# A list scheduler's prices are made anew: a port that GpSimd and VectorE share, waits within an engine, and TensorE's changes of shape

## The chip, the core and the metric

The kernel runs on one core of one Trainium2 chip. A core has a TensorE (PE) for matmuls, which writes only to PSUM; a VectorE (DVE), a ScalarE (ACT) and a GpSimd (POOL) for the rest of the arithmetic; and a SyncE (SP), which here issues every DMA. Each engine works through its own instructions in the order in which the program gives them, and semaphores hold an instruction until what it needs is there. The metric is the device time of one run of the whole program in microseconds, as the median of several runs.

## The reference

A two-layer trunk over 2048 latent tokens and 256 context tokens of width 1024, all in float32. Layer 0 has gated linear attention (GLA, chunks of 64, both directions) beside a gated linear recurrence (RG-LRU); layer 1 has windowed attention beside a chunked retention. Cut to its core:

```python
for i in range(DEPTH):                                   # 2 layers
    mod = silu(c) @ ada_w[i] + ada_b[i]                  # shift, scale and gate; the same map for c_ctx
    hl = rms_norm(x, norm_g[i]) * (1 + sc_l) + sh_l      # latent tokens
    hc = rms_norm(ctx_h, norm_g[i]) * (1 + sc_c) + sh_c  # context tokens
    if i % 2 == 0:                                       # GLA || RG-LRU
        q, k, v, g_gla, lr, xr, g_lru = split_cols(h @ w_in, EVEN_SIZES)
        b = cumsum(log_sigmoid(lr @ gla_up + gla_b) / 16) # within a chunk, both directions
        att = where(mask, (q * exp(b)) @ (k * exp(-b)).T, 0)
        S = decay[..., None] * S + k_st.T @ v             # from chunk to chunk
        o = att @ v + (q * exp(b)) @ S
        xc = conv(xr); r, ig = sigmoid(xc @ wa), sigmoid(xc @ wx)
        h_t = a_t * h_{t-1} + sqrt(1 - a_t**2) * ig * xc  # a = exp(8 r log_sigmoid(lam))
    else:                                                # windowed attention || retention
        p = softmax([q @ k.T in a window of +-128, q @ kc.T, sink]);  o = p @ [v, vc]
        o_ret = the chunked form above with one fixed decay for each head
    y = concat(branch outputs * silu(gates))
    x = x + g_l * (y @ w_out)
    ctx_h = ctx_h + g_c * (y_c @ w_out)                  # after layer 0 only
out = rms_norm(x, final_g)
```

## The kernel before

The tokens go through in five pieces, 256 of the context and four times 512 latent ones. For each layer and piece there are an input projection, the two branches, and an output projection. The projections are most of TensorE's work: `fm_block` (its matmul is L1148) and `tm_tiles` (L1169) run them as float32r matmuls of a 128 by 128 operand on 256 columns, three for each product, since weights and activations are split into a high part and a rest. A weight piece comes by DMA as raw float32 (`wr`, three buffers), ACT copies it to `wh` (L1051), and POOL or, for every fourth piece, DVE subtracts to get the rest `wl` (L1052); five buffers each of `wh` and `wl`. There are 496 such pieces.

Between the projections stand matmuls and transposes of other shapes, which use only a part of the 128x128 array:

- L1201, the conditioning for later stages (`ada_steps`), 128 matmuls with an output of 32 partitions;
- L1464, L1483 and L1503 of a GLA head (`gla_head`): chunk states with 64 input partitions, scores and the state's share of the output with 64 output partitions. L1500 is a matmul of the full shape into the same PSUM bank as L1503;
- L2145, L2194 of a retention head (`ret_kt`, `ret_head`): transposes and scores over 64 input partitions; L1857 and L2459, the corrections of later sweeps, likewise.

A float32 matmul is one instruction of the program and two in the trace.

In a GLA head DVE carries the states from chunk to chunk: L1470 for the forward direction on partitions 0 to 63, L1476 for the backward one on 64 to 127, up to eight steps each. Other chains on DVE that PE waits for: L1276 scales a row of tokens by its norm before the transposes L1321; L1437 makes the keys that L1446 transposes; L1493 makes the masked scores for L1500. In layer 1, L2010 and L2007 are the products of the rotary embedding, on DVE and on POOL.

**What sets the order.** No line of the kernel is issued in the order in which it is written. `Recorder` notes each call as an operation in `Plan.ops`; `touch` finds what it depends on; `cost` gives it a price in ns, as a pair of how long it occupies its engine and after how long its result is there; `wait` adds what a reader on another engine, or on the same one, sees on top. `ranks` computes for every operation the longest priced path to the end. `order` then plays the program through once: it takes the engine that is free first, and of the operations that are ready there the one of highest rank, gives it a buffer of its ring (tiles and PSUM banks are taken here), and sets its start. `emit` writes the operations out by these starts. So the planner's prices decide which instruction stands before which on each engine, and nothing else: at run time each waits only for its semaphores.

In the planner of before, PE has no price for a change of shape; a matmul over 64 partitions occupies PE three quarters as long as a full one. A later operation of the same engine that reads a result sees its latency with nothing added. DVE and POOL are independent. `touch` keeps the four groups of 32 partitions apart, and takes a PSUM bank as a whole.

Of the kernel before, what the change touches and what calls it, by code (L numbers as in the profile page):

```python
# [30 lines left out]
PE, ACT, DVE, POOL, SP = range(5)  # L31
KEEP = 99
# [83 lines left out]
class Buffer:  # L116
    def __init__(self, ring, seq, at):
        self.ring, self.seq, self.at = ring, seq, at
        self.spans = Spans(ring.cols * 4)
        self.users = []  # L120
        self.slot = self.tile = None


class Plan:
# [37 lines left out]
    def add(self, eng, fn, args, kw, after=(), line=None):  # L162
# [6 lines left out]
        for x in ins:  # L169
            self.touch(x, op, False, deps, takes)  # L170
        for x in outs:
            self.touch(x, op, True, deps, takes)
# [7 lines left out]
    def touch(self, ap, op, write, deps, takes):  # L180
# [66 lines left out]
    def cost(self, eng, name, out, ins, kw):  # L247
        if name == "preload_act_table_set":
            return 1290.0, 1290.0
# [5 lines left out]
        if eng == SP:  # L255
            return 430.0, 4.0 * out.shape[0] * n
        if eng == PE:
            if name == "transpose":
                return 112.0, 285.0
# [4 lines left out]
            if rhs.dtype == F32R:  # L264
                return max(120.0, 13.0 + cols / 2.35), 185.0 + cols / 2.4
            t = 2 * max(112.0, 5.0 + 2 * cols / 2.4)
            if lhs.shape[0] <= 64 or lhs.shape[-1] <= 64:
                t *= 0.75
            return t, t + 180.0
        if eng == DVE:  # L270
            if name == "tensor_tensor_scan":
# [9 lines left out]
            return t, t + 86.0  # L281
        if eng == ACT:
            t = (51.0 if ps else 93.0) + 0.833 * n + 94.0 * ptr
            return t, t + 100.0
        if name == "memset":
            return 40.0 + 0.9 * n, 110.0 + 0.9 * n
        if kw.get("op") == ALU.pow:
            return 370.0 + 152.0 * n, 440.0 + 152.0 * n
        if name == "tensor_scalar":
            return 270.0, 270.0  # L290
        t = 145.0 + 2.13 * n
        return t, t + 65.0


    def wait(self, j, e):

        f = self.ops[j][0]
        occ, lat = self.ops[j][6]
# [21 lines left out]
    def ranks(self, succ):  # L320
# [10 lines left out]
        for i in range(n - 1, -1, -1):  # L331
            occ, lat = self.ops[i][6]
# [13 lines left out]
    def order(self, key):  # L346
# [9 lines left out]
        dma = 0.0  # L356
# [79 lines left out]
        while count < n:  # L436
# [16 lines left out]
            i = heapq.heappop(now[e])[1]  # L453
            if ops[i][7]:
# [13 lines left out]
            occ, lat = ops[i][6]  # L468
# [2159 lines left out]
```

## Time and profile before

| | before |
|---|---|
| median of 3 timed runs | 2617.12 us (2615.71 to 2617.24) |
| the profiled execution, whole | 2622.66 us |
| its span, first to last instruction | 2620.9 us |
| PE busy | 2333.5 us, 89% |
| DVE busy | 1795.7 us, 69% |
| ACT busy | 1275.4 us, 49% |
| POOL busy | 807.7 us, 31% |
| mean granted clock of PE, as a share of full speed | 0.944 |
| matmul instructions in the trace | 17017 |
| of them projections (L1148, L1169) | 12216 |

A busy share adds up the spans of an engine's instructions. Matmuls overlap, so a matmul's own duration (0.28 us for a full one) is longer than the distance to the next one's start; what a matmul costs is read from the distances between starts. A wait in the profile names the operation that ended it, and the idle time before it. The granted clock is the share of pulses that PE was given in a stretch; it has two levels, 1.2 GHz (0.5) and 2.4 GHz (1.0).

### The profile page before, as it was taken

To read this page: it belongs to the slowest core of one execution; us is meant where nothing else is said; L and a number is where in the kernel's file an instruction comes from. 1 tells how busy PE (TensorE), PEld (TensorE's weight loads), DVE (VectorE), ACT (ScalarE), POOL (GpSimd) and SP (SyncE) were. 2 spreads that over 40 slices of the span, in tenths; PEclk is the share of its full clock that TensorE was granted. 3 is DMA by queue.
4 is the path that set the end of the run, shared out by engine and by line. 5 is a ranking of instruction groups with operands and counts; after the bars stand their busy time and mean duration, and the time that the engine had idled before them with its cause. 6 is when DMAs were issued, how large, how long until landed. Compare 5 with 4: busy or idle time off the path is not lost. (4 is left out here: it accounts for less than half of the span.)

```text
span 2620.9 us, 46207 instructions
## 1 busy us (share of the span) xinstructions
PE 2333.5 (89%) x17017; PEld 2095.8 (80%) x17017; DVE 1795.7 (69%) x3518; ACT 1275.4 (49%) x2721; POOL 807.7 (31%) x740
## 2 busy tenths in 40 slices
PE   6998779998997988788998889979999899899898
PEld 2987668677776878687888879978888788898898
DVE  3465676597569678647675687667777656777775
ACT  2363655465356456535234544455445543555553
POOL 1212213232233222334343234222343222323243
PEclk7998989998998999898999999989999899899999
DMA  7233334353443334665344254424444223425764
GB/s 219 65 102 108 110 107 110 106 152 106 122 124 99 108 82 129 214 202 171 90 131 134 87 160 125 139 90 125 124 135 147 75 85 98 148 81 178 253 221 137
DMA packets 372628, 340.67 MB, mean 130 GB/s; under 512 B 41832, under 2 KB 318768, under 8 KB 372400
## 3 DMA queue, kind: packets, MB, share of 16 engines
q1 hardware_dynamic: 372400, 337.71, 43.2%
q8 instruction: 133, 2.18, 0.4%
q14 instruction: 95, 0.78, 0.1%
HBM read 256.31 MB, written 67.67 MB: 124 GB/s over the span
## 5 line engine op out<-in xcount | busy, mean ns | idle before, releaser
L1169 PE MATMUL psum<-wh,ya 128*128 128x256 f32 x4416 | 909.9, 294 | 36.5 <-DVE tmp L2503 7.5
L1052 POOL TENSOR_TENSOR wl<-wr,wh 128x512 fp32r<-128x512 f32 x372 | 529.0, 1428 | 1202.2 <-ACT wh L1051 975.8
L1148 PE MATMUL psum<-ya,wh 128*128 128x256 f32 (+1 forms) x3728 | 785.3, 295 | 32.9 <-DVE tmp L1653 13.4
L1169 PEld LDWEIGHTS psum<-wh,ya 128*128 128x128 f32 x4416 | 711.2, 194 | 65.0 <-issue 12.2
L1148 PEld LDWEIGHTS psum<-ya,wh 128*128 128x128 f32 (+1 forms) x3728 | 609.7, 194 | 62.4 <-issue 23.6
L1169 PE MATMUL psum<-wl,ya 128*128 128x256 f32 x2208 | 581.2, 293 | 7.8 <-POOL wl L1052 3.9
L1148 PE MATMUL psum<-ya,wl 128*128 128x256 f32 (+1 forms) x1864 | 518.3, 296 | 3.7 <-DVE wl L1052 3.3
L1051 ACT CAST wh<-wr 128x512 fp32r<-128x512 f32 x496 | 302.5, 617 | 411.8 <-PE psum L1148 137.3
L1169 PEld LDWEIGHTS psum<-wl,ya 128*128 128x128 f32 x2208 | 402.2, 194 | 18.6 <-issue 5.5
L1148 PEld LDWEIGHTS psum<-ya,wl 128*128 128x128 f32 (+1 forms) x1864 | 348.9, 194 | 18.7 <-issue 11.0
L1052 DVE TENSOR_TENSOR wl<-wr,wh 128x512 fp32r<-128x512 f32 x124 | 97.1, 783 | 98.1 <-ACT wh L1051 85.1
L2010 DVE TENSOR_TENSOR tmp<-tmp,ub 32x512 f32<-32x512 f32 x144 | 146.7, 1019 | 20.7 <-ACT tmp L2352 10.3
L2093 PE MATMUL psum<-c_k_ident,ub 128*128 128x128 f32 x624 | 135.2, 283 | 16.8 <-DVE ub L2072 8.6
L2095 ACT CAST ur<-psum 128x512 fp32r<-128x512 f32 (+1 forms) x184 | 94.2, 521 | 101.4 <-PE psum L2093 95.3
L2068 ACT ACTIVATE ub<-ub,s_mx 128x640 f32<-128x640 f32 (+1 forms) x128 | 104.7, 818 | 78.7 <-DVE s_mx L2059 77.9
L2059 DVE CUSTOM_DVE_ANT_0 ub<-psum,uc 128x640 f32<-128x640 f32 (+2 forms) x128 | 108.2, 845 | 49.7 <-PE psum L2054 40.8
L2096 DVE TENSOR_TENSOR ur<-psum,ur 128x512 fp32r<-128x512 f32 (+1 forms) x184 | 109.6, 604 | 43.8 <-ACT ur L2095 42.9
L1328 DVE TENSOR_SCALAR tm<-psum,aT,shT 128x128 f32<-128x128 f32 x216 | 77.5, 403 | 35.5 <-PE psum L1321 17.5
L2093 PEld LDWEIGHTS psum<-c_k_ident,ub 128*128 128x128 f32 x624 | 80.2, 143 | 26.9 <-DVE ub L2072 15.1
L1321 PE MATMUL psum<-c_k_ident,xt 128*128 128x128 f32 x256 | 48.0, 315 | 39.5 <-DVE xt L1276 34.8
L2072 DVE TENSOR_SCALAR ub<-ub,s_rs 128x640 f32<-128x640 f32 (+1 forms) x128 | 78.7, 652 | 1.5
L1580 ACT ACTIVATE ub<-psum,gb 128x512 f32<-128x512 f32 (+3 forms) x96 | 52.6, 584 | 52.4 <-PE psum L1579 49.6
(321 smaller groups left out, 3943.2 us busy)
## 6 DMA issues: line engine op xcount, KB each, us to landing
wr<-in_o_w_in_dram SPq DMA_DIRECT2D x192, 256.0 KB, 3.0
wr<-in_e_w_in_dram SPq DMA_DIRECT2D x160, 256.0 KB, 3.0
wr<-in_e_w_out_dram SPq DMA_DIRECT2D x80, 256.0 KB, 3.3
tmp<-gl SPq DMA_DIRECT2D x64, 256.0 KB, 3.5
wr<-in_o_w_out_dram SPq DMA_DIRECT2D x64, 256.0 KB, 3.4
x1l<-tmp SPq DMA_DIRECT2D x40, 256.0 KB, 3.1
xt<-x1l SPq DMA_DIRECT2D x20, 512.0 KB, 4.2
ua<-in_ada_w_dram SPq DMA_DIRECT2D x32, 256.0 KB, 4.7
```

The costliest lines, as they stand in the source:

```text
L1051: S.copy(h[:, 0:n], raw[:, 0:n])
L1052: eng.tensor_tensor(l[:, 0:n], raw[:, 0:n], h.bitcast(F32)[:, 0:n], op=ALU.subtract)
L1148: T.matmul(ps[0:m, hf * HB:hf * HB + HB], lhsT=a, rhs=b, start=(hf == 0 and k == 0 and i == 0), stop=(hf == n // HB - 1 and k == 7 and i = ...
L1169: T.matmul(ps, lhsT=a, rhs=b, start=(ti % 2 == 0 and k == 0 and i == 0), stop=((ti % 2 == 1 or ti == len(tiles) - 1) and k == 7 and i == 2))
L1328: V.tensor_scalar(tm[:, kk], src, sc, sh, op0=ALU.mult, op1=ALU.add)
L2010: V.tensor_tensor(rot.v[to], raw.v[fr], sinb.v[fr], op=ALU.mult)
L2059: V.tensor_tensor_reduce(out=P_[:, c0:c0 + cn], in0=sc[:, so + c0:so + c0 + cn], in1=mask[:, m0:m0 + cn], scale=1.0, scalar=m, op0=ALU.add ...
L2068: tab_act(EXP, out=Ps[h], in_=Ps[h], func=AF.Exp, scale=-1.0, bias=mx[:, h:h + 1], accum_out=sm[:, h:h + 1])
L2072: PNORM.tensor_scalar(Ps[h], Ps[h], rs[:, h:h + 1], None, op0=ALU.mult)
L2093: T.transpose(tr[:, i * 256 + h * 128:i * 256 + h * 128 + 128], Ps[h][:, kb * 128:kb * 128 + 128], ident)
L2095: S.copy(ph[:, 0:n], tr[:, 0:n])
L2096: V.tensor_tensor(pl[:, 0:n], tr[:, 0:n], ph.bitcast(F32)[:, 0:n], op=ALU.subtract)
```

## The change

The prices and the planner's rules are changed, and no operation: the same instructions are recorded with the same operands. The parts are

1. **Shapes of TensorE.** `cost` gives each PE operation a kind: FULL, TR (large transposes), SMALL (64 or fewer input or output partitions), QUAD (32 or fewer output partitions). In `order`, leaving QUAD takes 500 ns more, leaving SMALL 200, entering either 90; after TR the next one comes up to 82 earlier. While the last operation was SMALL or QUAD and another of that kind is ready, that one is taken, whatever its rank.
2. **A port.** Operations of DVE that touch SBUF alone (more than one column, no reciprocal and no memset) and POOL's arithmetic have the kind PORT; only one of them runs at a time, the other is put back until the port is free, and its engine takes other work.
3. **Waits within an engine** (`SELF`): 33 ns on DVE, 25 on ACT, 40 on POOL are added when an operation reads a result of its own engine.
4. **Dependences.** With `FINE = False` all partitions of a column count as one; a PSUM bank is followed column by column, and PE's writes to one bank keep their order.
5. **Prices:** 470 ns for an SP issue (430), 93 ns more for an ACT instruction with an accumulated output, small corrections for matmuls.

```diff
+SELF = {DVE: 33.0, ACT: 25.0, POOL: 40.0}
+FULL, TR, SMALL, QUAD, PORT = range(1, 6)
+FINE = False
...
-        mask = sum(1 << q for q in range(4) if p0 < 32 * q + 32 and p1 > 32 * q)
+        mask = sum(1 << q for q in range(4) if p0 < 32 * q + 32 and p1 > 32 * q) if FINE else 15
...
-            if b.ring.psum:
-                sp.access(0, b.ring.cols * 4, 15, op, write, deps)
-                return
+            if b.ring.psum and write and eng == PE:
+                if b.last is not None:
+                    deps.setdefault(b.last, False)
+                b.last = op
...
             if name == "transpose":
-                return 112.0, 285.0
+                big = ins[0].shape[0] > 64 and ins[0].shape[-1] > 64
+                return (110.0, 285.0, TR) if big else (215.0, 300.0, SMALL)
...
+            if lhs.shape[0] <= 64 or lhs.shape[-1] <= 64:
+                if lhs.shape[-1] <= 32:
+                    return 0.1 * cols, 300.0 + 1.3 * cols, QUAD
+                t = max(112.0, 5.0 + 2 * cols / 2.4)
+                return t, t + 280.0, SMALL
             t = 2 * max(112.0, 5.0 + 2 * cols / 2.4)
-            if lhs.shape[0] <= 64 or lhs.shape[-1] <= 64:
-                t *= 0.75
-            return t, t + 180.0
+            return t, t + 180.0, FULL
         if eng == DVE:
+            kind = PORT if not ps and n > 1 and name not in ("reciprocal", "memset") else 0
...
         if e == f:
-            return lat if e in (DVE, ACT, POOL) else 0.0
+            return lat + SELF.get(e, 0.0) if e in SELF else 0.0
...
             i = heapq.heappop(now[e])[1]
+            if e == PE and last in (SMALL, QUAD) and ops[i][6][2] != last:
+                same = min((x for x in now[e] if ops[x[1]][6][2] == last), default=None)
+                if same:
+                    now[e].remove(same)
+                    now[e].append((key[i], i))
+                    heapq.heapify(now[e])
+                    i = same[1]
+            if ops[i][6][2] == PORT and port > t:
+                free[e] = t
+                heapq.heappush(later[e], (port, i))
+                continue
...
+            if kind == PORT:
+                port = t + occ
+            elif e == PE and kind != last:
+                if last == QUAD:
+                    t += 500.0
+                elif last == SMALL:
+                    t += 200.0
+                elif kind in (SMALL, QUAD):
+                    t += 90.0
+                elif last == TR:
+                    t -= min(82.0, max(0.0, t - at[i]))
+                last = kind
```

How the instructions stand on an engine is shown at three places. The changed file is 34 lines longer at these lines, so L1201 of before is L1235 of after, L1148 is L1182, L1169 is L1203, L2145 is L2179, L1470 is L1504 and L1476 is L1510.

TensorE in layer 0, where the conditioning (L1201, with an output of 32x256) meets the projections of the first latent pieces; before:

```order
L1201 MATMUL psum<-wh_1889,uc 32x256
L1169 MATMUL psum<-wh_1909,ya 128x256
L1169 MATMUL psum<-wl_1926,ya 128x256
L1169 MATMUL psum<-wh_1909,ya 128x256 x2
L1169 MATMUL psum<-wl_1926,ya 128x256
L1201 MATMUL psum<-wh_1889,uc 32x256
L1169 MATMUL psum<-wh_1909,ya 128x256 x2
L1169 MATMUL psum<-wl_1926,ya 128x256
L1201 MATMUL psum<-wl_1894,uc 32x256
L1169 MATMUL psum<-wh_1909,ya 128x256 x2
L1201 MATMUL psum<-wl_1894,uc 32x256
```

The same step of the conditioning on TensorE after:

```order
L1182 MATMUL psum<-ya,wh_1883 128x256 x2
L1182 MATMUL psum<-ya,wl_1893 128x256
L1235 MATMUL psum<-wh_1909,uc 32x256 x2
L1235 MATMUL psum<-wl_1913,uc 32x256 x2
L1235 MATMUL psum<-wh_1929,uc 32x256 x2
L1235 MATMUL psum<-wl_1939,uc 32x256 x2
L1203 MATMUL psum<-wh_1936,ya 128x256
```

The eight matmuls of one conditioning step stood apart, one or two at a time, and now stand in one row.

TensorE in layer 1, at the transposes of a retention head's keys (L2145) in a latent piece; before:

```order
L2145 MATMUL psum<-c_k_ident,ub 128x64
L1169 MATMUL psum<-wl_15135,ya 128x256
L1148 MATMUL psum<-ya,wh_15047 128x256
L2145 MATMUL psum<-c_k_ident,ub 128x64
L1169 MATMUL psum<-wh_15118,ya 128x256
L1148 MATMUL psum<-ya,wl_15057 128x256
L2202 MATMUL psum<-ub,uc 128x128
L2145 MATMUL psum<-c_k_ident,ub 128x64
```

At such transposes after:

```order
L2237 MATMUL psum<-uc 128x128
L2179 MATMUL psum<-c_k_ident,ub 128x64 x4
L2228 MATMUL psum<-ub 128x128 x4
L1203 MATMUL psum<-wl_15315,ya 128x256
L1203 MATMUL psum<-wh_15232,ya 128x256 x2
```

The four transposes stand together, with the four score matmuls of a head (L2194 of before) behind them, before the projection goes on.

VectorE in layer 0, at the two state chains of a GLA head (L1470 and L1476, into `ub`); before:

```order
L1470 SCALAR_TENSOR_TENSOR ub<-ub,s_dec_4914,psum 64x128
L1276 TENSOR_SCALAR xt_4743<-xt_4743,s_rstd_4989 128x1024
L1470 SCALAR_TENSOR_TENSOR ub<-ub,s_dec_4914,psum 64x128
L1476 SCALAR_TENSOR_TENSOR ub<-ub,s_dec_4914 64x128
L1470 SCALAR_TENSOR_TENSOR ub<-ub,s_dec_4914,psum 64x128
L1476 SCALAR_TENSOR_TENSOR ub<-ub,s_dec_4914 64x128
L1470 SCALAR_TENSOR_TENSOR ub<-ub,s_dec_4914,psum 64x128
L1476 SCALAR_TENSOR_TENSOR ub<-ub,s_dec_4914 64x128
```

At the same chains after:

```order
L1504 SCALAR_TENSOR_TENSOR ub<-ub,s_dec_4880,psum 64x128
L1589 COPY xcar<-ua_137 128x4
L1504 SCALAR_TENSOR_TENSOR ub<-ub,s_dec_4880,psum 64x128 x4
L1310 TENSOR_SCALAR xt_4762<-xt_4762,s_rstd_5026 128x1024
L1504 SCALAR_TENSOR_TENSOR ub<-ub,s_dec_4880,psum 64x128
L1616 TENSOR_TENSOR ub<-ub 128x512
L1504 SCALAR_TENSOR_TENSOR ub<-ub,s_dec_4880,psum 64x128
L1510 SCALAR_TENSOR_TENSOR ub<-ub,s_dec_4880 64x128
L1086 TENSOR_TENSOR wl_5069<-wr_4969,wh_5043 128x512
L1510 SCALAR_TENSOR_TENSOR ub<-ub,s_dec_4880 64x128
```

The steps of the two directions alternated; now the forward chain (L1504) comes first and the backward one behind it, and on both sides other work stands between some of the steps.

## Rows read from the trace of the kernel before

**Rows 1.** The page, its first part: busy time, share and instructions of PE.

```profile
PE 2333.5 (89%) x17017; PEld 2095.8 (80%) x17017; DVE 1795.7 (69%) x3518; ACT 1275.4 (49%) x2721; POOL 807.7 (31%) x740
```

**Rows 2.** The chain of waits at its end: start us, length us, what.

```profile
2571.79 35.71 PE psum L1169 x300
```

**Rows 3.** Timeline of PE, layer 0: start us, length us, line, names, shapes, count.

```profile
231.60 0.62 PE L1201 MATMUL psum<-wl,uc 128*32 128x256 f32 x2
232.15 0.39 PE L1169 MATMUL psum<-wl,ya 128*128 128x256 f32 x1
232.38 0.40 PE L1169 MATMUL psum<-wh,ya 128*128 128x256 f32 x2
232.71 0.62 PE L1201 MATMUL psum<-wh,uc 128*32 128x256 f32 x2
```

**Rows 4.** Timeline of PE, layer 0, sixteen matmuls of L1201 together.

```profile
351.39 0.41 PE L1201 MATMUL psum<-wh,uc 128*32 128x256 f32 x2
...
352.39 0.39 PE L1169 MATMUL psum<-wh,ya 128*128 128x256 f32 x1
352.62 0.28 PE L1169 MATMUL psum<-wl,ya 128*128 128x256 f32 x1
```

**Rows 5.** Timeline of PE, layer 0, a lone pair of L1483.

```profile
426.62 0.43 PE L1483 MATMUL psum<-ub,uc 128*64 128x128 f32 x2
426.99 0.39 PE L1169 MATMUL psum<-wh,ya 128*128 128x256 f32 x1
427.21 0.40 PE L1169 MATMUL psum<-wl,ya 128*128 128x256 f32 x2
427.54 0.43 PE L1483 MATMUL psum<-ub,uc 128*64 128x128 f32 x2
```

**Rows 6.** Timeline of PE, layer 0, eight matmuls of L1483 together.

```profile
155.32 0.28 PE L1577 MATMUL psum<-ur 128*128 128x256 f32 x1
155.53 0.66 PE L1483 MATMUL psum<-ub,uc 128*64 128x128 f32 x8
156.11 0.51 PE L1148 MATMUL psum<-ya,wh 128*128 128x256 f32 x2
156.45 0.29 PE L1578 MATMUL psum<-ur 128*128 128x256 f32 x1
```

**Rows 7.** Timeline of PE, layer 1, transposes L2145 one at a time.

```profile
1309.77 0.27 PE L2145 MATMUL psum<-c_k_ident,ub 64*128 64x64 f32 x1
1309.97 0.50 PE L1148 MATMUL psum<-ya,wh 128*128 128x256 f32 x2
1310.40 0.27 PE L2145 MATMUL psum<-c_k_ident,ub 64*128 64x64 f32 x1
```

**Rows 8.** Line L2010: shortest, median and longest duration in ns.

```profile
L2010 DVE TENSOR_TENSOR tmp<-tmp,ub x144: 678/686/1762, 1218.4 to 2362.6; 32x512 f32<-32x512 f32 x144
```

**Rows 9.** The page, its costliest groups: busy us, mean ns, idle before, releaser.

```profile
L1052 POOL TENSOR_TENSOR wl<-wr,wh 128x512 fp32r<-128x512 f32 x372 | 529.0, 1428 | 1202.2 <-ACT wh L1051 975.8
...
L2010 DVE TENSOR_TENSOR tmp<-tmp,ub 32x512 f32<-32x512 f32 x144 | 146.7, 1019 | 20.7 <-ACT tmp L2352 10.3
```

**Rows 10.** Waits of PE: for whom, us in total, times, longest us.

```profile
PE psum L1321 <- DVE xt L1276: 34.8, 17, 6.0
PE psum L1500 <- DVE uc L1493: 20.5, 11, 3.9
...
PE psum L1446 <- DVE uc L1437: 16.6, 8, 4.7
```

**Rows 11.** Timeline of DVE in a GLA head of layer 0, two steps of the chains.

```profile
135.00 0.34 DVE L1470 SCALAR_TENSOR_TENSOR ub<-ub,s_dec,psum 64x128 f32<-64x128 f32 x1
135.37 0.35 DVE L1476 SCALAR_TENSOR_TENSOR ub<-ub,s_dec 64x128 f32<-64x128 f32 x1
```

**Rows 12.** Timeline of PE, layer 0: in brackets the idle time before, and its releaser.

```profile
361.44 0.58 PE L1208 MATMUL psum<-sel,uc 128*128 128x2 f32 x2 [5.58 <-DVE uc L1204]
```

**Rows 13.** Busy us and instructions of each engine in a stretch, then PE's granted clock.

```profile
359.00:376.00 17.00, 9.80 (x48) 8.51 (x49) 15.28 (x55) 8.03 (x24) 3.71 (x6) 0.51 0.22 59
```

More of the change, by code (lines that the diff above doesn't have):

```diff
@@ L120, in __init__ @@
         self.users = []
-        self.slot = self.tile = None
+        self.slot = self.tile = self.last = None
 class Plan:
@@ L169, in add @@
         for x in ins:
-            self.touch(x, op, False, deps, takes)
+            self.touch(x, op, eng, False, deps, takes)
         for x in outs:
-            self.touch(x, op, True, deps, takes)
+            self.touch(x, op, eng, True, deps, takes)
         deps.pop(op, None)
@@ L178, in add, with touch @@
         return op
-    def touch(self, ap, op, write, deps, takes):
+    def touch(self, ap, op, eng, write, deps, takes):
         t = ap.tensor
@@ L248, in cost @@
         if name == "preload_act_table_set":
-            return 1290.0, 1290.0
+            return 1290.0, 1290.0, 0
         n = 1
@@ L255, in cost @@
         if eng == SP:
-            return 430.0, 4.0 * out.shape[0] * n
+            return 470.0, 4.0 * out.shape[0] * n, 0
         if eng == PE:
             if name == "transpose":
-                return 112.0, 285.0
+                big = ins[0].shape[0] > 64 and ins[0].shape[-1] > 64
+                return (110.0, 285.0, TR) if big else (215.0, 300.0, SMALL)
             lhs, rhs = kw["lhsT"], kw["rhs"]
@@ L264, in cost @@
             if rhs.dtype == F32R:
[L265 removed]
+                return max(118.0, 12.0 + cols / 2.38), 185.0 + cols / 2.4, FULL
+            if lhs.shape[0] <= 64 or lhs.shape[-1] <= 64:
[3 more added lines that the diff above has]
+                return t, t + 280.0, SMALL
             t = 2 * max(112.0, 5.0 + 2 * cols / 2.4)
[L267 to L269 removed]
+            return t, t + 180.0, FULL
         if eng == DVE:
+            kind = PORT if not ps and n > 1 and name not in ("reciprocal", "memset") else 0
             if name == "tensor_tensor_scan":
@@ L280, in cost @@
                 t = 66.0 + 60.0 * (ptr if name in ("tensor_scalar", "scalar_tensor_tensor") else 0) + 1.045 * n
-            return t, t + 86.0
+            return t, t + 86.0, kind
         if eng == ACT:
             t = (51.0 if ps else 93.0) + 0.833 * n + 94.0 * ptr
-            return t, t + 100.0
+            if "accum_out" in kw:
+                t += 93.0
+            return t, t + 100.0, 0
         if name == "memset":
-            return 40.0 + 0.9 * n, 110.0 + 0.9 * n
+            return 40.0 + 0.9 * n, 110.0 + 0.9 * n, 0
         if kw.get("op") == ALU.pow:
-            return 370.0 + 152.0 * n, 440.0 + 152.0 * n
+            return 370.0 + 152.0 * n, 440.0 + 152.0 * n, PORT
         if name == "tensor_scalar":
-            return 270.0, 270.0
+            return 270.0, 270.0, PORT
         t = 145.0 + 2.13 * n
-        return t, t + 65.0
+        return t, t + 65.0, PORT
     def wait(self, j, e):
         f = self.ops[j][0]
-        occ, lat = self.ops[j][6]
+        occ, lat, _ = self.ops[j][6]
         if f == SP:
@@ L331, in ranks @@
         for i in range(n - 1, -1, -1):
-            occ, lat = self.ops[i][6]
+            occ, lat, _ = self.ops[i][6]
             r = occ
@@ L355, in order @@
         free = [0.0] * 5
-        dma = 0.0
+        dma, port, last = 0.0, 0.0, 0
         key = key(self, succ)
@@ L467, in order @@
                     wake(b.ring)
-            occ, lat = ops[i][6]
+            occ, lat, kind = ops[i][6]
+            if kind == PORT:
[10 more added lines that the diff above has]
+                last = kind
             start[i], done[i] = t, True
```

## The prediction

> **What bounds the kernel now.** I read the page's busy shares first, then TensorE's (PE's) matmuls one by one in the order of time, then what PE waits for. PE is busy 2333.5 of 2620.9 us, 89% [rows 1]; no other engine is over 69%. It is idle 287 us. Where nothing holds it, one 128x256 matmul of a projection (L1148, L1169) starts every 35.71 / 300 = 0.119 us [rows 2]. So a cost that the busy share hides is seen by comparing distances between starts with 0.119.
>
> Such a cost stands at changes of shape. L1201 (the conditioning, output of 32 partitions) stands in pairs between projection matmuls: from 231.60 to 232.71 lie one pair and three projection matmuls, 1.11 us; less 3 x 0.119 that is 0.75 us for the pair [rows 3]. Where sixteen of L1201 stand together (eight rows of two), the time from the first to the second projection matmul behind is 352.62 - 351.39 = 1.23 us [rows 4], against 232.38 - 231.60 = 0.78 us for a pair [rows 3]: fourteen more cost 0.45, or 0.032 us each. So the pair itself is 0.07 and each visit to this shape costs 0.68 us whatever its length. L1483 (GLA, 64 output partitions) says the same: a lone pair with three projection matmuls takes 0.92 us, so 0.56 for the pair [rows 5]; eight together, from 155.32 to 156.45 with three others, take 1.13, so 0.77 for the eight [rows 6], 0.035 each: a visit costs 0.49. A lone transpose of 64 partitions (L2145) and two projection matmuls take 0.63 us [rows 7], so 0.39 for the transpose; even if 0.119 of that is its own work, the visit costs 0.27.
>
> **The change part by part.**
>
> *Fewer changes of shape.* Counting in both orders each place where a matmul of a smaller shape follows one of another shape: L1201 goes from 79 visits to 24; L1483 from 55 to 20 and L1503 from 104 to 72 (both 64 output partitions); L2145 from 59 to 17; the other matmuls over 64 input partitions (L1464, L1857, L2194, L2459) together from 112 to 54. Priced: 55 x 0.68 = 37.4 us; 67 x 0.49 = 32.8; 42 x 0.27 = 11.3; 58 at between 0.27 and 0.49, of which I take the middle, 0.38 = 22.0. Sum 103.5 us (97 to 110 by the two ends) off PE's own time. The instructions are the same ones, so nothing is added against it.
>
> How much of that is off the path? PE is idle 11% of the span [rows 1]; there a matmul that ends sooner only makes PE wait longer. I count that share twice, since a shorter PE will meet more inputs that are not there yet, and let 0.8 through: 83 us. The ends are 0.3 (the stages with most small shapes are also those where chains on VectorE set the pace) and 1.0. What is late next are the inputs from VectorE (DVE) that head PE's waits [rows 10].
>
> Against letting it through speaks a rule: the Trainium skill (TensorEngine Tiling, section Performance Considerations, PSUM Bottleneck) says that faster work on small tiles does not make the emptying of PSUM any faster, which can become the bound. By that rule nothing would come through where the emptying decides, and the sum would keep only the next term; no row here shows how far that goes.
>
> *The shared port.* DVE's rope products L2010 take 686 ns in the median and up to 1762 [rows 8], 1019 in the mean over 144 [rows 9]: 48 us over the median, at lengths that one GpSimd (POOL) instruction of 1.4 us explains. POOL's weight splits L1052 take 1428 ns in the mean [rows 9]. The changed planner lets such work of the two engines exclude each other, so DVE's row is filled with work on PSUM meanwhile. On the path this counts only where PE waits for DVE work that touches SBUF alone: 34.8 us for L1276, 20.5 for L1493, 16.6 for L1437 [rows 10], 71.9 together. Most of each is the chain itself, not the port. I take a quarter, 18 us, with 0 and 36 as ends on the good side; it can also go below nothing by as much, -18, because a port operation that the planner holds back may be the one that PE needs.
>
> *Waits within an engine.* The two state chains of GLA (L1470 on partitions 0 to 63, L1476 on 64 to 127) stood alternately, and now stand one after the other. A step starts 0.37 us after the one before although the two touch different partitions [rows 11], so alternation hid nothing and its loss costs nothing. Sixteen steps are 6 us either way; the old planner, which took the chains as independent and a step as 0.26 to 0.35, thought them shorter. In the orders DVE waits for the instruction just before it 262 times before and 286 after; 24 waits of some 0.1 us are 2 us on an engine that is 31% idle: nothing.
>
> *The rest.* The 40 ns more for each DMA issue, the reader's part of an accumulating ACT instruction, the column-wise PSUM dependence and the coarse partition masks change no instruction. They only make the planner's clock nearer to the chip's; I give them nothing in the sum and hold them for the first rival.
>
> Sum on the profiled execution: 2620.9 + 1.8 around the span = 2622.7; less 83 and 18 is 2521.7. The median of the timed runs, 2617.1, lies 5.5 us under that execution, so the forecast is **2516 us**, 3.9% less.
>
> **The rivals.**
>
> *A: PE's stalls shrink as well.* A planner that knows what the chip does places inputs in time everywhere. If a third of the 287 us idle goes (96 us) and all of the 103.5 comes through: 2622.7 - 103.5 - 96 - 5.5 = 2418. The clock would help: from 359 to 376 us PE, which had stood idle for 5.58 us until 361.44 [rows 12], had a granted clock of 0.51, so mostly the lower of its two levels, and started 48 matmuls in 17 us [rows 13], 2.8 a us against 8.4 in [rows 2]. The Trainium skill (TensorE: Matmul & The Clock Gate, section Why this matters for your kernels) says that idle gaps between bursts put the engine on its lower rate; by that rule each stall avoided pays twice, and the trace agrees in this stretch. Against it: the schedule is still a greedy one, and the order within layers is anew at every place, for better or worse. Chance 0.16.
>
> *B: the gain is eaten.* 136 of the 222 visits saved are of layer 0, where ACT and DVE chains of GLA and RG-LRU run beside the projections. If 0.3 of the 103.5 comes through and the port gives nothing: 2622.7 - 31 - 5.5 = 2586. For it: the waits of [rows 10] on L1493 and L1437 are all of that layer. Against it: PE is busy 89% overall. Chance 0.21.
>
> *C: slower, by late weight splits.* Every projection matmul needs a piece that POOL or DVE has split (L1052), and 372 of the 496 are POOL's. The planner now refuses a POOL split the port while DVE's SBUF work holds it, and on POOL's queue all later splits stand behind. The 12216 matmuls of L1148 and L1169 use 496 pieces, so a piece feeds 24.6 of them, 2.9 us of PE; five pieces are held, some 12 us of lead with one in use. If splits fall behind by more than that lead, PE waits on each; at 0.35 us a split (a quarter of its 1.43 us) that is 372 x 0.35 = 130 us, more than the 83 saved: 2622.7 - 83 + 130 - 5.5 = 2664. Against it: POOL was idle 1202 us before these splits, 976 of them waiting for ACT's copy [rows 9], so it seldom is the late one. Chance 0.08.
>
> *D: no change.* The plan is followed as an order only, and a better price for PE need not move the end. But the visits are gone from the order, which the planner's estimate cannot undo; time within 0.2% would need the waits to grow by just what is saved. Chance 0.03.
>
> **How the numbers follow.** The forecast has 0.52, with a range of its own from 2478 (all of the 103.5 and 36 for the port: 2622.7 - 139.5 - 5.5) to 2565 (half of the 103.5 and nothing else: 2622.7 - 52 - 5.5). A's 2418 is the middle of a case that begins at 2478, so a bound of 2430 takes in about half of it and leaves 0.08 out; B's 2586 lies inside a bound of 2592, which leaves out some 0.05 of it and all of C. So the range is 2430 to 2592, with about 0.2 outside. Faster by over 0.2% (about what a measurement of this kernel can tell from no change): 0.52 + 0.16 + 0.21 = 0.89; within 0.2%: 0.03; slower: 0.08.
>
> **What would show it.** Right: L1201 in runs of eight whose whole visit is near 1 us; L2145 in fours; PE's idle time near 290 to 310 us with its busy time some 90 to 100 us less; no PE wait for L1052 over 15 us. Rival A shows as PE idle time under 220 us and a higher mean granted clock; rival B as idle time over 340 us, with the waits of [rows 10] longer; rival C as PE waiting for POOL's L1052 by tens of us. The prediction is wrong at its root if the fixed cost of a visit stays with the long visits (sixteen of L1201 then cost far over 1.3 us), or if small matmuls taken early wait for inputs and hold PE.

## The result, and the profile after

The changed kernel takes 2502.09 us in the median (2498.79 to 2503.43), beside 2616.41 us for the kernel before on the same chip: a ratio of 0.9563 (95% interval 0.9546 to 0.958), 4.4% faster. The prediction said 2516 us, in a range of 2430 to 2592. The total was close. Two of the terms that make it up were not: the experiments below show that the port is worth about three times what was forecast for it, and the shapes less.

L1276 of before, too, stands 34 lines further on: it is L1310 now. First the page of the kernel after, its busy times, beside [rows 1].

```profile
span 2501.6 us, 46111 instructions
...
PE 2218.4 (89%) x17017; PEld 2046.1 (82%) x17017; DVE 1773.4 (71%) x3518; ACT 1277.1 (51%) x2721; POOL 797.3 (32%) x740
```

PE's busy time fell by 2333.5 - 2218.4 = 115.1 us; its idle time went from 287.4 to 2501.6 - 2218.4 = 283.2 us. DVE is busy 22 us less. The mean granted clock is 0.945, where it was 0.944.

The shapes now stand together. PE's timeline shows sixteen matmuls of L1235 in one visit (start us, length us, line, names, shapes, count).

```profile
213.52 0.41 PE L1235 MATMUL psum<-wh,uc 128*32 128x256 f32 x2
213.53 0.41 PE L1235 MATMUL psum<-wl,uc 128*32 128x256 f32 x2
...
214.52 0.39 PE L1203 MATMUL psum<-wh,ya 128*128 128x256 f32 x1
214.75 0.28 PE L1203 MATMUL psum<-wl,ya 128*128 128x256 f32 x1
```

From the first of them to the second projection matmul behind it lie 214.75 - 213.52 = 1.23 us, just what such a group of before took [rows 4]; eleven visits of the kernel after hold sixteen, where before had four. The fixed price doesn't grow with the length of the visit. L2179 stands in fours at most places.

```profile
1513.06 0.46 PE L2179 MATMUL psum<-c_k_ident,ub 64*128 64x64 f32 x4
1513.45 0.39 PE L1182 MATMUL psum<-ya,wh 128*128 128x256 f32 x1
1513.68 0.28 PE L1182 MATMUL psum<-ya,wl 128*128 128x256 f32 x1
```

Here 0.62 us hold four transposes and one projection matmul; less 0.119, four cost 0.50, where one alone cost 0.39 [rows 7].

What PE waits for (for whom, us in total, times, longest us), beside [rows 10]:

```profile
PE psum L1537 <- DVE ub L1510: 20.5, 9, 7.1
PE psum L2087 <- DVE s_mx L2093: 16.6, 21, 1.7
...
PE psum L1355 <- DVE xt L1310: 11.1, 9, 3.0
...
PE psum L1203 <- DVE wl L1086: 5.1, 4, 4.3
PE psum L1203 <- POOL wl L1086: 3.8, 3, 1.5
...
PE psum L1534 <- DVE uc L1527: 0.7, 1, 0.7
```

The three waits of [rows 10] shrank, that for L1276 (now L1310) from 34.8 to 11.1 us and that for L1493 (now L1527) from 20.5 to 0.7. In their place stands one for the backward chain of GLA, L1510, of 20.5 us (L1476 before, 2.0 us). The weight splits (L1086) are not late.

Two groups of the page, beside [rows 9]: busy us and mean ns, then the idle time before.

```profile
L1086 POOL TENSOR_TENSOR wl<-wr,wh 128x512 fp32r<-128x512 f32 x372 | 519.5, 1403 | 939.7 <-ACT wh L1085 817.6
...
L2044 DVE TENSOR_TENSOR tmp<-tmp,ub 32x512 f32<-32x512 f32 x144 | 135.4, 942 | 17.9 <-ACT tmp L2386 7.2
```

The rope products on DVE (L2010, now L2044) take 942 ns in the mean, from 1019.

### The profile page after: what moved, and what is told of

Same layout as the page of the kernel before. It is cut to its first block, busy times and chain, and to the rows that moved or that the text cites. A ratio compares the mean times of both kernels' runs of the same rounds, so it can differ in the third digit from the quotient of the medians.

```text
span 2501.6 us, 46111 instructions
## 1 busy us (share of the span) xinstructions
PE 2218.4 (89%) x17017; PEld 2046.1 (82%) x17017; DVE 1773.4 (71%) x3518; ACT 1277.1 (51%) x2721; POOL 797.3 (32%) x740
## 5 line engine op out<-in xcount | busy, mean ns | idle before, releaser
L1203 PE MATMUL psum<-wh,ya 128*128 128x256 f32 x4416 | 871.9, 291 | 35.5 <-DVE tmp L1677 12.0
L1086 POOL TENSOR_TENSOR wl<-wr,wh 128x512 fp32r<-128x512 f32 x372 | 519.5, 1403 | 939.7 <-ACT wh L1085 817.6
L1182 PE MATMUL psum<-ya,wh 128*128 128x256 f32 (+1 forms) x3728 | 752.9, 292 | 40.5 <-DVE tmp L1687 11.6
L1203 PEld LDWEIGHTS psum<-wh,ya 128*128 128x128 f32 x4416 | 697.7, 193 | 51.2 <-ACT wh L1085 10.9
L1182 PEld LDWEIGHTS psum<-ya,wh 128*128 128x128 f32 (+1 forms) x3728 | 603.3, 194 | 56.7 <-DVE tmp L1687 13.8
L1203 PE MATMUL psum<-wl,ya 128*128 128x256 f32 x2208 | 569.0, 290 | 9.1 <-DVE wl L1086 5.1
L1182 PE MATMUL psum<-ya,wl 128*128 128x256 f32 (+1 forms) x1864 | 514.9, 291 | 1.9 <-DVE wl L1086 1.9
L1203 PEld LDWEIGHTS psum<-wl,ya 128*128 128x128 f32 x2208 | 398.2, 194 | 13.6 <-DVE wl L1086 7.0
L1182 PEld LDWEIGHTS psum<-ya,wl 128*128 128x128 f32 (+1 forms) x1864 | 351.5, 194 | 7.6 <-issue 3.7
L2044 DVE TENSOR_TENSOR tmp<-tmp,ub 32x512 f32<-32x512 f32 x144 | 135.4, 942 | 17.9 <-ACT tmp L2386 7.2
L1086 DVE TENSOR_TENSOR wl<-wr,wh 128x512 fp32r<-128x512 f32 x124 | 89.3, 720 | 63.2 <-ACT wh L1085 62.1
L1291 POOL TENSOR_TENSOR s_rstd<-s_rstd,mhalf 128x1 f32<-128x1 f32 (+2 forms) x88 | 73.2, 835 | 5.8
L2106 DVE TENSOR_SCALAR ub<-ub,s_rs 128x640 f32<-128x640 f32 (+1 forms) x128 | 73.4, 608 | 1.2
```

The costliest lines, as they stand in the source:

```text
L1086: eng.tensor_tensor(l[:, 0:n], raw[:, 0:n], h.bitcast(F32)[:, 0:n], op=ALU.subtract)
L1182: T.matmul(ps[0:m, hf * HB:hf * HB + HB], lhsT=a, rhs=b, start=(hf == 0 and k == 0 and i == 0), stop=(hf == n // HB - 1 and k == 7 and i = ...
L1203: T.matmul(ps, lhsT=a, rhs=b, start=(ti % 2 == 0 and k == 0 and i == 0), stop=((ti % 2 == 1 or ti == len(tiles) - 1) and k == 7 and i == 2))
L2044: V.tensor_tensor(rot.v[to], raw.v[fr], sinb.v[fr], op=ALU.mult)
L2106: PNORM.tensor_scalar(Ps[h], Ps[h], rs[:, h:h + 1], None, op0=ALU.mult)
```

## The experiments

Two theories were put to the test. **V**: the whole gain is the fixed price of visits to a smaller shape. **P**: the planner's other parts, the port above all, gain a share of their own, by fewer stalls. The change falls into three parts that can be undone one by one (part P is the port alone, while theory P takes the port and the waits together): **S**, TensorE's kinds, prices, switch costs and the rule that stays with a shape; **P**, the port; **W**, the waits within an engine, the dependences and the two small prices. The edits on the kernel after:

Without S:

```diff
-            if e == PE and last in (SMALL, QUAD) and ops[i][6][2] != last:
-                same = min((x for x in now[e] if ops[x[1]][6][2] == last), default=None)
...
-                if last == QUAD:
-                    t += 500.0
-                elif last == SMALL:
-                    t += 200.0
...
+            if lhs.shape[0] <= 64 or lhs.shape[-1] <= 64:
+                t *= 0.75
+            return t, t + 180.0, 0
```

Without P:

```diff
-            if ops[i][6][2] == PORT and port > t:
-                free[e] = t
-                heapq.heappush(later[e], (port, i))
-                continue
```

Without W:

```diff
-SELF = {DVE: 33.0, ACT: 25.0, POOL: 40.0}
+SELF = {DVE: 0.0, ACT: 0.0, POOL: 0.0}
...
-FINE = False
+FINE = True
...
-            if b.ring.psum and write and eng == PE:
...
+            if b.ring.psum:
+                sp.access(0, b.ring.cols * 4, 15, op, write, deps)
+                return
...
-            return 470.0, 4.0 * out.shape[0] * n, 0
+            return 430.0, 4.0 * out.shape[0] * n, 0
```

With the kernel before and the kernel after, six runs make all eight combinations. All of them issue the same instructions; only their order differs.

**S alone** (`shapes_only`: without P and W).

> The kernel after with everything of the change undone but TensorE's part: the port, the waits within an engine, the finer and coarser dependences and the two small prices are as before; the kinds, prices and switch costs of matmuls and the rule that stays with a shape are kept. Its order has 192 visits to a smaller shape (after 195, before 417). Theory V (the whole gain is the fixed price of visits, 115.1 us / 222 = 0.52 us each): 2502 us, within 10 of the kernel after. Theory P (port and waits give a part of their own, the prediction's 18 us): 2520 or more. A third way, that port and waits cost something: under 2490.

Measured: 2561.51 us, ratio 0.9768 (0.9744 to 0.9791). Theory V falls: the visits are as few as in the kernel after (192), and nearly half of the gain is missing.

```profile
PE 2232.6 (87%) x17017; PEld 2071.6 (81%) x17017; DVE 1814.0 (71%) x3518; ACT 1274.2 (50%) x2721; POOL 793.7 (31%) x740
```

PE is busy 100.9 us less than before, for 225 visits: 0.45 us each, close to the 0.47 of the prediction's sum. But it is idle 2558.0 - 2232.6 = 325.4 us, 38 more than before.

**P and W without S** (`no_shapes`).

> The kernel after with TensorE's part undone (old price of a matmul, no switch costs, no rule that stays with a shape), the port, the waits within an engine and the dependences kept. Its order has 347 visits (before 417, after 195). Theory V: only the 70 visits fewer than before count, 70 x 0.52 = 36 us, so 2580 us. Theory P (18 us or more from port and waits on top): 2562 or less. If port and waits cost something without the shapes: 2600 or more. TensorE's busy time by V: 2333 - 36 = 2297 us.

Measured: 2575.3 us, 0.9831 (0.9805 to 0.9856), between the two theories. PE is busy 2302.4 us (31 less, for 70 visits) and idle 266.4 (21 less).

**S and W without P** (`no_port`).

> The kernel after, but a port operation no longer waits in the plan for the other engine's. Visits as in after (194). Theory V: within 8 us of after's 2502. Theory P: 2511 to 2520, with the mean of L2044 on VectorE back from 942 ns towards 1019 and that of L1086 on VectorE from 720 towards 783.

Measured: 2537.8 us, 0.968 (0.9661 to 0.97): 36 us from the kernel after, at least twice what theory P expected. The mean of the rope products is back at 1016 ns and DVE's busy time at 1803.5 us; the splits on DVE went from 720 to 744 ns, not to 783.

**S and P without W** (`port_shapes`).

> The kernel after with the port and TensorE's part kept, and the waits within an engine, the dependences and the two small prices as before. 192 visits. If the port alone makes the second part of the gain (TensorE's part alone gave 2562, after 2502): 2500 to 2515 us. If waits within an engine and dependences make some 24 us of it, as the step from TensorE's part alone to the kernel without the port says: 2520 to 2535.

Measured: 2498.5 us, 0.9541 (0.9521 to 0.956). These two parts make the whole gain.

```profile
PE 2207.1 (89%) x17017; PEld 2049.4 (82%) x17017; DVE 1787.0 (72%) x3518; ACT 1275.1 (51%) x2721; POOL 799.0 (32%) x740
```

Beside S alone, with the same 192 visits, PE is idle 38.8 us less (286.6) and also busy 25.5 us less. The second number is the clock's: the granted clock is 0.943 here and 0.932 there. Pulses not granted come to 2558.0 x 0.068 = 174 us there and 2493.7 x 0.057 = 142 here, 32 us apart. Those that were not granted while PE was busy, worked out from all of PE's instructions and the trace's record of the clock, come to 135 us there and 105 here, 30 apart. So between these two orders each us of idle time avoided paid nearly twice. The Trainium skill (TensorE: Matmul & The Clock Gate, section Why this matters for your kernels) says that idle gaps between bursts bring the engine back to its lower rate, and these two traces agree with it.

**P alone** (`port_only`).

> The kernel after with everything undone but the port. 405 visits to smaller shapes (before 417). If the port is worth by itself what it is worth on top of TensorE's part (2562 to 2498.5, 63 us): 2550 us, with 6 us of that from the 12 visits. If the prediction's 18 us was right: 2595. If the port only gains where the shapes are gathered (it then keeps VectorE, which such gathering loads, from being late): 2610 or more. VectorE's busy time in the first case some 30 us under before's 1796.

Measured: 2541.79 us, 0.9684 (0.9662 to 0.9706), 3.2% faster with 405 visits, nearly all those of before. It is the largest of the single parts.

```profile
PE 2296.9 (91%) x17017; PEld 2071.6 (82%) x17017; DVE 1748.7 (69%) x3518; ACT 1276.5 (50%) x2721; POOL 792.8 (31%) x740
...
L2022 DVE TENSOR_TENSOR tmp<-tmp,ub 32x512 f32<-32x512 f32 x144 | 134.9, 937 | 27.0 <-ACT tmp L2298 19.0
```

DVE is busy 47 us less than before, PE is idle 47 us less (240.4), and the clock is 0.953, the highest of all runs. The rope products (here L2022) account for 12 of DVE's 47 us; the rest is spread over many lines.

**W alone** (`waits_only`).

> The kernel after without the port and without TensorE's part: the waits within an engine, the dependences and the two small prices alone. 360 visits, since the dependences let matmuls of one bank stand together. If only visits count, 57 x 0.52 = 30 us: 2590 us. If the waits are worth the 24 us between TensorE's part alone (2562) and the kernel without the port (2538) besides: 2566. If they are worth nothing and the visits saved do not come through: 2610 or more.

Measured: 2626.26 us, 1.0016 (1.0 to 1.0032): nothing, although 57 visits are gone and PE is busy 22 us less. It is idle 20 us more.

**Is it chance?** A list scheduler answers any change of a price with a new order at many places. Two controls move one price that tells it nothing new.

```diff
-                return max(118.0, 12.0 + cols / 2.38), 185.0 + cols / 2.4, FULL
+                return max(118.5, 12.0 + cols / 2.37), 185.0 + cols / 2.4, FULL
```

> The kernel after with one price moved by less than 1%: a projection matmul is planned at 118.5 ns and not 118, with a slope of 2.37 and not 2.38. Visits to smaller shapes as in after (195); the order of the projections is anew in many places. It tells how much of a difference between two orders is chance. If the 36 us between after and the kernel without the port, and the 24 us between that and the kernel with TensorE's part alone, are causes: within 8 us of after's 2502. If they are chance: 15 us or more away, to either side.

Measured: 2496.51 us, 0.9533 (0.9514 to 0.9552).

```diff
-        return t, t + 65.0, PORT
+        return t, t + 70.0, PORT
```

> The same test with another price: GpSimd's own wait for a result is planned 5 ns longer (latency 70 ns, not 65). Visits as in after (195). Causes: within 8 us of 2502. Chance: 15 us or more away.

Measured: 2506.96 us, 0.9568 (0.9546 to 0.9591). Both lie within 6 us of the kernel after. The differences of 36 to 82 us between the parts are far over that. How far chance moves an order without S or without P was not measured.

**Is it the port, or any spacing of GpSimd's work?** In `act_port` (P alone, otherwise) the planner keeps POOL apart from ScalarE's SBUF work instead of DVE's.

```diff
-            kind = PORT if not ps and n > 1 and name not in ("reciprocal", "memset") else 0
+            kind = 0
...
-            return t, t + 100.0, 0
+            return t, t + 100.0, 0 if ps else PORT
```

> The kernel with the port alone, but the planner excludes GpSimd's work with ScalarE's SBUF work instead of VectorE's. GpSimd's operations are held back in the same way, by another engine, one whose durations did not move between the kernels (the copies L1085 of ScalarE took 617 and 618 ns in before and after). 421 visits (before 417). If the port's 81 us come from keeping VectorE and GpSimd apart: nothing of them, 2610 to 2635 us, VectorE's busy time back near 1796 us or above. If they come from any rule that spaces GpSimd's work or makes the order anew: 2540 to 2570. If planned exclusion itself costs: over 2640.

Measured: 2637.54 us, 1.007 (1.0053 to 1.0086), 18 us slower than before and just over the 2635 us that the first case allowed. The execution profiled was the longest of the five (2653.95 us).

```profile
PE 2358.7 (89%) x17017; PEld 2114.1 (80%) x17017; DVE 1800.6 (68%) x3518; ACT 1272.5 (48%) x2721; POOL 799.0 (30%) x740
...
L2022 DVE TENSOR_TENSOR tmp<-tmp,ub 32x512 f32<-32x512 f32 x144 | 149.4, 1038 | 15.9 <-ACT tmp L2298 8.7
```

DVE's busy time and the rope products are back near the values of before or over them. The same rule on the wrong pair gains nothing; it is the pair DVE and POOL that counts.

**A visit's price from the other side.** In `scatter` the planner leaves a smaller shape as soon as a full matmul is ready.

```diff
-            if e == PE and last in (SMALL, QUAD) and ops[i][6][2] != last:
-                same = min((x for x in now[e] if ops[x[1]][6][2] == last), default=None)
+            if e == PE and last in (SMALL, QUAD) and ops[i][6][2] == last:
+                same = min((x for x in now[e] if ops[x[1]][6][2] == FULL), default=None)
```

> The kernel after with the rule turned round: behind a matmul of a smaller shape the planner takes a full one, if one is ready. 767 visits, against 195 in after, the same instructions. By the prices of [rows 3 to 7] (117 of L1235 at 0.68 for 24, 144 and 137 of L1517 and L1537 at 0.49 for 20 and 72, 72 of L2179 at 0.27 for 17, 289 others at 0.38 for 54): 63 + 93 + 15 + 89 = 260 us more busy time on TensorE, and 2700 to 2765 us if 0.75 to 1.0 of it comes through. If visits cost little by themselves and the gain was one of the order: under 2600.

Measured: 2796.87 us, 1.0678 (1.066 to 1.0696), some 295 us over the kernel after and 32 over the range expected.

```profile
PE 2569.7 (92%) x17017; PEld 2192.7 (78%) x17017; DVE 1753.7 (63%) x3518; ACT 1280.5 (46%) x2721; POOL 787.0 (28%) x740
```

PE is busy 351 us more for 572 visits and idle 59 us less (224.4), so the time grew by 0.83 of it. It is 91 us more than the prices of the rows make. The granted clock is 0.913, though PE is idle less than in any other run: pulses not granted come to 2794.1 x 0.087 = 243 us, against 2501.6 x 0.055 = 138 in the kernel after, 105 us more. All of that fell while PE was busy (212 us beside 101). Without it the visits cost 241 us, 0.42 each, a little under the 260 of the rows. So PE's idle time does not explain this clock; that the visits themselves lower it fits, but no run isolates it.

**Fewer visits still.** The 72 visits of L1537 that stay in the kernel after come of alternating L1534 (full) with L1537 in one PSUM bank. `gla` records the four L1534 first.

```diff
-            T.matmul(op_[:, o], lhsT=bdm[:, t], rhs=vt.v[:, t, 128 * j:128 * j + 128], start=True, stop=False)
+            T.matmul(op_[:, o], lhsT=bdm[:, t], rhs=vt.v[:, t, 128 * j:128 * j + 128], start=(t == 0), stop=False)
+        for t in range(p.nt):
+            o = slice(t * 128, t * 128 + 128)
             for cc in range(2):
...
-                         start=False, stop=True)
+                         start=False, stop=(t == p.nt - 1))
```

> The kernel after, but the four full-shape matmuls L1534 of a GLA head's output are recorded ahead of its eight L1537 (64 output partitions), where they alternated. Visits go from 195 to 150, those of L1537 from 72 to 20, those of L1517 from 20 to 24. Theory V by the price of [rows 5, 6]: 48 x 0.49 = 23.5 us off TensorE's busy time and, with the share that came through in the change (1.0), 2478 us. If what stands behind is VectorE's or ScalarE's chain of layer 0 (rival B's mechanism): busy time 23 us less, but 2495 to 2505 us.

Measured: 2501.62 us, 0.9542 (0.9523 to 0.956), the same as the kernel after within the intervals. PE is busy 2200.1 us, 18.3 less, and idle 298.5, 15.3 more. The waits say where it went:

```profile
PE psum L1480 <- DVE uc L1471: 22.7, 6, 6.2
...
PE psum L1203 <- DVE wl L1086: 12.9, 8, 5.4
```

L1480 (the transposes of GLA's keys, L1446 before) waits 22.7 us for DVE, 5.3 in the kernel after; the weight splits 12.9, from 5.1. In the first layer DVE's chains are what is late next.

The same edit on S and P without W:

> Port and TensorE's part alone, as in the run of that kind (2498.5 us), and the full-shape matmuls of a GLA head's output recorded ahead of its eight with 64 output partitions. 146 visits (192 there). 46 x 0.49 = 22.5 us less busy time. If it comes through: 2476 us. If layer 0 waits for VectorE's chains, as the first such run (2501.6) says: 2490 to 2500, with TensorE idle 10 us or more longer.

Measured: 2491.6 us, 0.9489 (0.9463 to 0.9515), the fastest version of the study. It beats the kernel before by 5.1% and, by the ratios to before on two chips, the kernel after by some 0.8%. Its busy time fell by only 8.9 us beside S and P, and the profiled executions of the two are as long (2493.0 and 2493.7 us of span), so that the edit on GLA gives those 0.5% is not shown by the trace.

## All eight combinations, and where the two gains lie

"DVE held" adds up, over the groups of equal DVE instructions, by how much each is longer than the median of those in its group that meet no POOL instruction. It was worked out from all of DVE's instructions of a trace. "Not granted" is the time of the pulses that were not granted while PE was busy. Gains are against before, as a share of 2620 us.

| parts | visits | ratio | gain, us | PE busy | PE idle | DVE busy | DVE held | clock | not granted |
|---|---|---|---|---|---|---|---|---|---|
| none (before) | 417 | 1 | 0 | 2333.5 | 287.4 | 1795.7 | 231 | 0.944 | 117 |
| W | 360 | 1.0016 | -4 | 2311.5 | 307.2 | 1801.0 | 235 | 0.942 | 117 |
| S | 192 | 0.9768 | 61 | 2232.6 | 325.4 | 1814.0 | 251 | 0.932 | 135 |
| S, W | 194 | 0.968 | 84 | 2229.9 | 305.9 | 1803.5 | 241 | 0.938 | 121 |
| P | 405 | 0.9684 | 83 | 2296.9 | 240.4 | 1748.7 | 187 | 0.953 | 84 |
| P, W | 347 | 0.9831 | 44 | 2302.4 | 266.4 | 1766.3 | 197 | 0.942 | 111 |
| S, P | 192 | 0.9541 | 120 | 2207.1 | 286.6 | 1787.0 | 226 | 0.943 | 105 |
| S, P, W (after) | 195 | 0.9563 | 114 | 2218.4 | 283.2 | 1773.4 | 209 | 0.945 | 101 |

Each part is added in four places of this table. S gives 61, 88, 37 and 70 us, 64 in the mean. P gives 83, 48, 59 and 30, 55 in the mean. W gives -4, 23, -39 and -6, -6 in the mean. DVE is held less in each of the four pairs with P, by 44, 38, 25 and 32 us, though most of it stays; in `act_port` it is about 234 us, as in before.

S and P gain mostly at different places: together they give 120 of the 144 us that each gives alone. The windows below cut each trace behind its first 5,000 matmuls (all in layer 0) and behind its first 15,000; columns are window, its length, busy us and instructions of each engine, PE's granted clock, DMA share and GB/s. Before:

```profile
0.00:841.00 841.00, 733.56 (x5009) 599.02 (x5011) 545.26 (x1124) 419.75 (x720) 203.45 (x210) 0.92 0.41 117
841.00:2340.00 1499.00, 1345.12 (x10000) 1250.81 (x9997) 1055.94 (x1991) 714.40 (x1564) 502.43 (x426) 0.95 0.42 126
```

S alone:

```profile
0.00:794.00 794.00, 672.01 (x5001) 584.96 (x5002) 545.74 (x1122) 417.52 (x718) 194.40 (x209) 0.90 0.43 124
794.00:2279.00 1485.00, 1307.04 (x10005) 1241.03 (x10004) 1071.16 (x1993) 715.99 (x1567) 498.41 (x427) 0.94 0.43 127
```

P alone:

```profile
0.00:828.00 828.00, 726.18 (x5002) 596.66 (x5002) 530.41 (x1129) 420.71 (x719) 200.85 (x209) 0.92 0.42 119
828.00:2260.00 1432.00, 1316.02 (x10003) 1229.73 (x10002) 1025.41 (x1986) 714.89 (x1565) 488.58 (x425) 0.97 0.44 131
```

After:

```profile
0.00:776.00 776.00, 658.77 (x5003) 573.02 (x5003) 542.99 (x1131) 419.28 (x720) 197.49 (x209) 0.92 0.44 128
776.00:2225.00 1449.00, 1307.60 (x10002) 1228.55 (x10001) 1035.49 (x1984) 715.68 (x1564) 494.53 (x425) 0.95 0.44 130
```

In the first stretch S takes 61.6 us off PE's busy time and 47 off the stretch: 0.76 comes through. In the second it takes 38 off the busy time and 14 off the stretch: 0.37, since PE's idle time there grows from 154 to 178 us. P is the reverse: 13 us of the first stretch, 67 of the second, where PE's idle time falls from 154 to 116 us; the other 29 us are busy time, at a clock of 0.97 for 0.95. Of the idle time I added up what DVE ends: 117 us before, 85 with P, 127 with S. What ACT ends is 29.5, 28.6 and 48. In the second stretch PE is 90% busy, and yet DVE's lengths decide what P gains.

The second stretch still holds the end of layer 0's branches. Cut once more behind the last L1503 (L1530 in S alone), it reads, before:

```profile
841.00:1069.00 228.00, 205.29 (x1522) 181.59 (x1519) 174.46 (x315) 135.49 (x245) 71.34 (x53) 0.94 0.39 109
1069.00:2340.00 1271.00, 1139.83 (x8479) 1069.21 (x8480) 881.48 (x1677) 578.91 (x1320) 431.09 (x373) 0.95 0.43 128
```

S alone:

```profile
794.00:1028.00 234.00, 201.06 (x1533) 184.13 (x1531) 183.75 (x321) 137.08 (x248) 66.54 (x54) 0.91 0.39 108
1028.00:2279.00 1251.00, 1105.97 (x8473) 1056.89 (x8473) 887.40 (x1673) 578.91 (x1319) 431.87 (x373) 0.95 0.43 130
```

At the end of layer 0's branches S takes 4 us off the busy time, and the stretch grows by 6. Behind it 20 of 34 us come through, 0.59. Layer 0's branches as a whole pass on 41 of 66, 0.62: nearly the same share.

One meeting of DVE and POOL, in before's timeline. Met by a weight split of POOL:

```profile
1441.34 1.28 POOL L1052 TENSOR_TENSOR wl<-wr,wh 128x512 fp32r<-128x512 f32 x1
1441.39 1.78 DVE L1276 TENSOR_SCALAR xt<-xt,s_rstd 128x1024 f32<-128x1024 f32 x1
...
1443.32 0.74 PE L1321 MATMUL psum<-c_k_ident,xt 128*128 128x128 f32 x5 [0.81 <-DVE xt L1276]
```

The same instruction in the same trace, with no POOL instruction beside it:

```profile
1171.99 0.75 DVE L1276 TENSOR_SCALAR xt<-xt,s_rstd 128x1024 f32<-128x1024 f32 x1 [0.93 <-POOL s_rstd L1257]
```

DVE's instruction began 0.05 us behind POOL's and took 1.78 us where it takes 0.75, and PE stood idle 0.81 us for it. The Trainium skill (SBUF — State Buffer, section SBUF: two separate sides) calls the shared port pair an exclusive lock that is held for a whole instruction. By that DVE would wait until 1442.62 and end at 1443.37; it ended at 1443.17, so the trace agrees to 0.2 us. The Trainium skill also says, in the same section, that ScalarE never waits there; its copies took 617 ns in the mean before and 618 after, and excluding it gained nothing (`act_port`).

## Why the prediction was right, and where it was not

**Visits and their price: right.** 222 visits less and 103.5 us off PE's own time were forecast. S alone, with 225 less, takes 100.9 us off the busy time, the kernel after 115, S and P together 126. These differ in part by the clock: with the pulses not granted while PE was busy taken out, they are 119, 99 and 114 us, and the forecast lies among them.

**The share that comes through: too high.** The step put 0.8 of it, 83 us, on the path. S alone gained 61 of 101, which is 0.60, and 37 us on top of P, where it takes 90 us off the busy time. It gave 64 us in the mean of its four places. Two things took the rest. One is late inputs. The step named those from DVE, but with S alone, where PE is idle 38 us more, ACT ends 23 us more of the idle time and DVE 20 (other releasers a little less); on top of P it is idle 46 us more, all of it ended by DVE. The other is the clock, which the step left out: S alone lost 18 us more of busy time to pulses not granted than before, so that 119 us of work gone show as 101 of busy time. Nor is layer 0 the place, as the text feared for its lower end: its branches passed on 0.62 and what follows 0.59. Inside layer 0 it varied, 0.76 in the first stretch and nothing at the end. How much of the late inputs is the emptying of PSUM, which the prediction names, no run separates.

**The port: about three times too low.** 18 us were forecast, 36 as the good end. Its measured worth is 30 to 83 us, 55 in the mean; on top of S and W, the lowest of the four, it stays within the good end. The term was sized from three waits of PE [rows 10] and a quarter of them, on the ground that only where PE waits for SBUF-only work of DVE does the port count. But L1276, the first of them, met POOL nearly as often after (13 of 36 instructions over 1.3 us, 12 before). DVE is one queue: holds gone anywhere on it bring forward all that stands behind them, PSUM work included, and in the later stretch DVE ended 117 of PE's 154 idle us. With P alone DVE is held 44 us less, and what DVE ends of PE's idle time falls by 43 us over the whole trace (209 to 166). Most of what P alone gains beyond that is the clock's, which the term had not at all: 33 us fewer were lost to pulses not granted while PE was busy. DVE's whole lengthening, 231 us before, was the number to start from. I had it in hand for L2010 alone (48 us over the median).

**The two errors offset each other.** 83 + 18 = 101 us forecast, 114 measured, as 64 + 55 - 6 of means. The total was right with two of its terms wrong, which is luck, and without undoing the parts one by one it would have looked like a confirmation of the visits.

**The waits within an engine and the rest: nothing, as put,** when alone (1.0016), and in the mean of four places. But W moves single pairs by -39 to +23 us, far over the 5 us of the two controls. Why it takes 39 us from P alone and gives 23 to S alone stays open.

**The signs that were named.** Right: L1235 in long visits, L2179 in fours, PE idle near 290 (283), no wait for the splits over 15 us (5.1 and 3.8). The busy time fell by 115 us, more than the 90 to 100 named. Rival A's signs did not come in the kernel after: 283 us idle, clock 0.945. Its mechanism is there, though, in P alone: idle 240 and 0.953. Its 2.8 matmuls a us were not the clock's alone, since PE was busy only 9.80 of those 17 us [rows 13]. Rival B's mechanism, the gain eaten by the chains of ACT and DVE, is part of what holds S alone at 61 us, and DVE's chains hold `gla` at nothing. Rival C (late splits) didn't occur; D was excluded by the visits, as argued.

## What to carry to other kernels

Where one engine is 90% busy, size an edit on another engine by what that engine ends of the first one's remaining idle time, stretch by stretch, and by all its lengthened instructions, not by the few waits at the head of the list. Keep VectorE's SBUF-only work and GpSimd's apart in the order, and gather TensorE's smaller shapes into long visits, since a visit's price doesn't depend on its length. Undo the parts of a change one by one, beside a control that only shuffles the order, before you believe the sum.

## What the runs showed of the hardware that was not expected

- The planned exclusion of VectorE and GpSimd, with no instruction changed, is worth 3.2% by itself (0.9684); the same exclusion of ScalarE and GpSimd costs 0.7% (1.007).
- Two orders with the same 192 visits differ by 25.5 us in PE's busy time, and the pulses not granted while PE was busy differ by 30 us (granted clock 0.932 and 0.943).
- The order with 767 visits has PE idle least (224.4 us) and yet the lowest granted clock, 0.913.
